# Seven quarter products for eight in the feed-forward stages of a two-block transformer kernel

## The chip, the cores and the metric

The kernel runs on one core of one Trainium2 chip. The metric is device time in microseconds, the median of three runs. The engines of the core are called PE (matrix products; PEld is its loading of weights), DVE (vector), ACT (scalar), POOL (GpSimd) and SP (which here only issues loads).

## The reference

A sequence of 512 tokens of width 1024 goes through two layers of a first block (mixer, then an MLP with a convolution and GELU) and two layers of a second one (feed-forward, mixer, feed-forward). The change is in the four feed-forward stages of the second block:

```python
D_FF_2 = 128 * ((8 * D_MODEL // 3 + 127) // 128)      # 2816

def swiglu(x, w_gate, w_up, w_down):
    return (jax.nn.silu(x @ w_gate) * (x @ w_up)) @ w_down

x = x + 0.5 * swiglu(rms_norm_2(x, norm_ffn1[l]), ffn1_w_gate[l], ffn1_w_up[l], ffn1_w_down[l])
x = x + hybrid_mixer(rms_norm_2(x, norm_mix[l]), ...)
x = x + 0.5 * swiglu(rms_norm_2(x, norm_ffn2[l]), ffn2_w_gate[l], ffn2_w_up[l], ffn2_w_down[l])
```

All of it is in fp32.

## The kernel before

Every dense product is made of three matmuls in float32r. Both operands are split in a high part (a copy rounded by ACT) and a low part (the rest, by DVE), and high x high, high x low and low x high are added up in PSUM (`mm3a`, `mm3b`).

Weights come through `Stream` in chunks of 128 x 1024, in the order of their use. SP loads a chunk into one of three raw buffers; ACT makes `whi` from it (L63), DVE makes `wlo` (L64), into one of four pairs of buffers. `release` frees the pair of a chunk that is used up and at once issues the split of the chunk four places ahead; that split waits until PE has read the old pair.

In a feed-forward stage, the activations lie feature-major in `H`, high and low, 8 blocks of 128 features by 512 tokens. `fm` takes one chunk for 128 output features: 8 blocks x 3 matmuls of 512 columns (L166 to L168). Chunks of gate and up alternate, 44 in all. The first four chunks are done in halves of 256 tokens, since the norm of the last tokens is not ready yet: first all four for tokens 0 to 255, then all four for the rest. `flush` issues, ahead of a half, what is pending for its tokens. `to_h` (L204) turns a token block of 128 by PE and splits it into `H`; block 2 is done as the first half goes on, block 3 at the boundary of the halves. After a gate chunk ACT applies SiLU (L433), after an up chunk DVE multiplies (L437), and the result is split at once into `hid` high and low (L426, L427). Then `finish` makes the down product token-major in two passes of 512 columns (`tm`, L172 to L174), with `hid` as the stationary operand.

The instruction streams of the engines are in the order in which the program issues them (a manual schedule), so whatever is issued to an engine waits for all that was issued to it before. In `fm` the order after a chunk is: evacuation first, then `release`. PSUM has two sets of four banks, tags "a" and "b".

Of the kernel before, what the change touches and what calls it, by code (L numbers as in the profile page):

```python
# [18 lines left out]
L = 2  # L19
# [13 lines left out]

MIX_ORDER = (4, 5, 0, 1, 2, 6, 7, 3)
# [3 lines left out]
class Stream:  # L38
    """Weights in the order of their use: each chunk is loaded, split in two
    float32r parts whose sum it is, and given out."""  # L40

    def __init__(self, nc, raw_pool, split_pool, n_raw, n_split):
        self.nc, self.raw_pool, self.split_pool = nc, raw_pool, split_pool
        self.n_raw, self.n_split = n_raw, n_split
        self.specs, self.raw, self.parts = [], {}, {}
        self.loaded = self.split = self.taken = 0
        self.done = set()
        self.oldest = 0

    def load_ahead(self):  # L50
        while self.loaded < len(self.specs) and self.loaded - self.split < self.n_raw:
            t = self.raw_pool.tile([128, CHUNK], F32, name="wraw")
            self.nc.sync.dma_start(t, self.specs[self.loaded])
            self.raw[self.loaded] = t
            self.loaded += 1

    def split_ahead(self):
        while self.split < len(self.specs) and self.split - self.oldest < self.n_split:
            self.load_ahead()
            t = self.raw.pop(self.split)  # L60
            hi = self.split_pool.tile([128, CHUNK], F32R, name="whi")
            lo = self.split_pool.tile([128, CHUNK], F32R, name="wlo")
            self.nc.scalar.activation(hi, t, AF.Copy)  # L63
            self.nc.vector.tensor_sub(lo, t, hi.bitcast(F32))  # L64
            self.parts[self.split] = (hi, lo)
            self.split += 1
            self.load_ahead()
# [24 lines left out]
class Block:  # L92
    def __init__(self, tc, ctx, a, out):
        self.tc, self.nc, self.a, self.out = tc, tc.nc, a, out
        pool = lambda name, bufs=1, **kw: ctx.enter_context(tc.tile_pool(name=name, bufs=bufs, **kw))
        self.const = pool("const")
        self.keep = pool("keep")
        self.small = pool("small", 4)
        self.gains = pool("gains", 2)
        self.sq = pool("sq", 1)  # L100
        raw, parts = pool("wraw", 3), pool("wparts", 4)
        self.psum = pool("psum", 4, space=bass.MemoryType.PSUM)
        ctx.enter_context(tc.manual_schedule())
# [4 lines left out]
        self.n_half = 4  # L108

# [59 lines left out]

    def mm3b(self, ps, h, w, first, last):  # L170
# [96 lines left out]
    def tm(self, nk, width, rows, evac, tag, tail=0, opens=False):  # L267
        """Token-major products: nk feature blocks against chunks of CHUNK // width
        blocks of width columns each."""
# [11 lines left out]
        for c in range(head):  # L281
# [4 lines left out]
            self.st.release(i)  # L286
        if head == n_chunks:
            for t in range(NT):
                evac(t, ps[t])
            return  # L290
        got = []
        for t in range(NT):
            if opens:
                self.flush(max(self.opened, t))
            for c in range(n_chunks - head):
# [5 lines left out]
                if t == NT - 1 and c == 0:  # L301
                    self.st.release(i)
            evac(t, ps[t])
# [4 lines left out]

    def finish(self, nk, rows, gain, scale=None, post=None, final=False):
        """x += the product of rows with the next weights (scaled, or normed with  # L310
        the gain post), then the next norm's rows on their way to self.H."""
# [40 lines left out]
        def normed(t):  # L352
# [3 lines left out]
            def rows_of_h():  # L356
# [4 lines left out]
                else:  # L361
                    self.later(1800 if t < NT - 1 else math.inf, t, lambda: self.to_h(t, parts, first))
# [3 lines left out]
        self.tm(nk, 512, rows, part0, first)  # L366
        if not final:
            self.new_h()
        self.tm(nk, 512, rows, part1, last, tail=3 if post is None else 4)
# [5 lines left out]
    def begin(self, gain):  # L375
        """The first norm, in the order in which tokens and weights arrive."""
# [95 lines left out]
    def ffn(self, l, next_gain, final):  # L472
        self.mlp(None, next_gain, final)

# [5 lines left out]
    def spare(self, name):  # L480
        """A scratch tile from the slots that the norms use between the stages."""
# [307 lines left out]
    def pooling(self, u, share, pw, gcols, mix):  # L789
        """Means over windows of 2 and 4, then 8 and 16 tokens, by halves."""  # L790
# [133 lines left out]
    def tokens(x, g, t):  # L924
        """The tokens of tile t of group g, of x [p, T]: a run of tokens, or the
        tokens that are t modulo 4, one or four whole residue classes."""
        return x[:, t::4] if g else x[:, t * 128:(t + 1) * 128]

    def dilated(self, half, fm, v, o_dil):
# [4 lines left out]
        for s in range(2):  # L934
# [6 lines left out]
            def near(i):  # L941
                """Scores of key blocks 2i and 2i + 1, each for its own and the next block."""
# [61 lines left out]
            # weights, numerators and denominators  # L1004
# [96 lines left out]
def body(ctx, tc, a, out, stages):  # L1101
    nc = tc.nc
    B = Block(tc, ctx, a, out)
    for kind, l in stages:
        B.st.specs += [a["w_" + kind][l, i] for i in range(N_CHUNKS[kind])]
# [6 lines left out]
    B.begin(gains[0])  # L1112
    for i, (kind, l) in enumerate(stages):
        with tc.tile_pool(name=f"ph{i}", bufs=1) as B.phase:
            f = B.ffn if kind in ("ffn1", "ffn2") else getattr(B, kind)
# [7 lines left out]
def constants():  # L1123
    """Tables that depend on the shapes alone."""
# [40 lines left out]
def tiles_a(w):  # L1165
    """[L, D, N] as chunks [L, N // 128, 128, 8 * 128] of whole columns."""
# [4 lines left out]
def tiles_b(w, width):  # L1171
    """[L, K, N] as chunks [L, (N // width) * (K // 128 // per), 128, per * width]."""
# [5 lines left out]
def arrange(inp):  # L1178
    """The inputs laid out as the program reads them."""
# [12 lines left out]
    def pairs(g, u):  # L1192
        return np.stack([tiles_a(g), tiles_a(u)], axis=2).reshape(L, 2 * KF, 128, CHUNK)
# [3 lines left out]
    for n in ("1", "2"):  # L1197
        a["w_ffn" + n] = np.concatenate([pairs(inp[f"ffn{n}_w_gate_2"], inp[f"ffn{n}_w_up_2"]),
# [43 lines left out]
```

## Time and profile before

| what | value |
|---|---|
| median of three runs | 3565.03 us (3563.9 to 3568.91) |
| span of the profiled execution, first to last instruction | 3553.4 us |
| that execution's own time | the page gives its span alone; the median is 11.6 us above it |
| PE busy | 3500.0 us (98%) |
| DVE, ACT, POOL busy | 43%, 33%, 10% |
| share of PE in the chain that ended last | 93% |

Times in rows are microseconds from the first instruction unless marked ns. A matmul's duration includes its way through the array, and consecutive ones overlap; the distance between starts is what a matmul takes from the next.

### The profile page before, as it was taken

To read this page: it belongs to the slowest core of one execution; us is meant where nothing else is said; L and a number is where in the kernel's file an instruction comes from. 1 tells how busy PE (TensorE), PEld (TensorE's weight loads), DVE (VectorE), ACT (ScalarE), POOL (GpSimd) and SP (SyncE) were. 2 spreads that over 40 slices of the span, in tenths; PEclk is the share of its full clock that TensorE was granted. 3 is DMA by queue.
4 is the path that set the end of the run, shared out by engine and by line. 5 is a ranking of instruction groups with operands and counts; after the bars stand their busy time and mean duration, and the time that the engine had idled before them with its cause. 6 is when DMAs were issued, how large, how long until landed. Compare 5 with 4: busy or idle time off the path is not lost.

```text
span 3553.4 us, 39868 instructions
## 1 busy us (share of the span) xinstructions
PE 3500.0 (98%) x16304; PEld 2842.4 (80%) x16304; DVE 1512.6 (43%) x1973; ACT 1163.3 (33%) x1854; POOL 351.3 (10%) x412
## 2 busy tenths in 40 slices
PE   8999999999999999999999999999999999999999
PEld 6678887767888788889887888888888988788887
DVE  4655542465554343324543533233332454353322
ACT  4344432334443232222235332222222223532222
POOL 2411100241110000002200100000000220010000
PEclk9999999999999999999999999999999999999999
DMA  4123232312223232222111232323222211123232
GB/s 154 47 73 101 95 107 78 110 48 73 100 95 108 76 102 94 101 101 88 49 60 60 89 102 94 104 86 101 94 100 97 88 48 60 61 90 104 92 104 77
DMA packets 87191, 312.00 MB, mean 88 GB/s; under 512 B 10369, under 2 KB 11073, under 8 KB 87009
## 3 DMA queue, kind: packets, MB, share of 16 engines
q1 hardware_dynamic: 85536, 305.17, 25.3%
q0 software_dynamic: 1472, 4.30, 0.4%
q8 instruction: 128, 2.10, 0.2%
q14 instruction: 55, 0.44, 0.0%
HBM read 307.32 MB, written 2.10 MB: 87 GB/s over the span
## 4 chain that ended last, share of the span: by engine, by line
PE 93%; DVE 3%; ACT 1%; POOL 1%; issue 1%; DMA 0%; DVEq 0%; SPq 0%; POOLq 0%; ACTq 0%
PE pa L166 19%; PE pa L167 18%; PE pa L168 18%; PE pb L172 10%; PE pb L173 10%; PE pb L174 10%; PE pst L932 1%; PE pz L1038 1%; PE psc L625 1%; DVE wlo L64 1%; PE ph L209 1%; PE pod L1026 1%; PE pos L1038 1%; PE po L661 1%; DVE pb L343 0%
## 5 line engine op out<-in xcount | busy, mean ns | idle before, releaser
L64 DVE TENSOR_TENSOR wlo<-wraw,whi 128x1024 fp32r<-128x1024 f32 x556 | 708.5, 1277 | 1207.0 <-ACT whi L63 1205.7
L166 PE MATMUL pa<-h_hi,whi 128*128 128x512 f32 (+1 forms) x3072 | 1180.7, 384 | 4.4 <-ACT h_hi L151 4.4
L167 PE MATMUL pa<-h_lo,whi 128*128 128x512 f32 (+1 forms) x3072 | 1158.6, 377 | 5.7 <-DVE h_lo L152 5.7
L168 PE MATMUL pa<-h_hi,wlo 128*128 128x512 f32 (+1 forms) x3072 | 1157.5, 377 | 0.0
L63 ACT ACTIVATE whi<-wraw 128x1024 fp32r<-128x1024 f32 x556 | 583.3, 1052 | 685.4 <-PE pb L174 516.8
L166 PEld LDWEIGHTS pa<-h_hi,whi 128*128 128x128 f32 x3072 | 578.5, 188 | 136.5 <-issue 16.0
L168 PEld LDWEIGHTS pa<-h_hi,wlo 128*128 128x128 f32 x3072 | 578.3, 188 | 117.8
L167 PEld LDWEIGHTS pa<-h_lo,whi 128*128 128x128 f32 x3072 | 579.0, 188 | 116.2 <-DVE h_lo L152 7.9
L172 PE MATMUL pb<-whi,hid_hi 128*128 128x512 f32 x1056 | 413.8, 392 | 0.0
L174 PE MATMUL pb<-whi,hid_lo 128*128 128x512 f32 x1056 | 413.0, 391 | 0.0
L173 PE MATMUL pb<-wlo,hid_hi 128*128 128x512 f32 x1056 | 413.0, 391 | 0.0
L174 PEld LDWEIGHTS pb<-whi,hid_lo 128*128 128x128 f32 x1056 | 198.1, 188 | 43.7
L173 PEld LDWEIGHTS pb<-wlo,hid_hi 128*128 128x128 f32 x1056 | 198.2, 188 | 43.6
L172 PEld LDWEIGHTS pb<-whi,hid_hi 128*128 128x128 f32 x1056 | 198.2, 188 | 43.0
L426 ACT ACTIVATE hid_hi<-act 128x512 fp32r<-128x512 f32 x88 | 55.7, 633 | 396.8 <-DVE act L437 396.8
L190 POOL TENSOR_TENSOR rs<-ss 128x1 f32<-128x1 f32 x44 | 8.8, 200 | 1635.7 <-ACT sqs L180 1635.7
L437 DVE TENSOR_TENSOR act<-act,pa 128x512 f32<-128x512 f32 x88 | 60.5, 688 | 223.3 <-PE pa L168 223.3
L172 PE MATMUL pb<-whi,h_hi 128*128 128x256 f32 (+1 forms) x384 | 142.3, 371 | 2.7 <-ACT whi L63 2.3
L173 PE MATMUL pb<-wlo,h_hi 128*128 128x256 f32 (+1 forms) x384 | 140.0, 365 | 3.9 <-DVE wlo L64 3.9
L446 DVE SCALAR_TENSOR_TENSOR cv<-pa,cw,cv 128x511 f32<-128x511 f32 (+1 forms) x176 | 131.5, 747 | 27.4 <-ACT cv L444 24.3
L174 PE MATMUL pb<-whi,h_lo 128*128 128x256 f32 (+1 forms) x384 | 139.4, 363 | 0.0
L433 ACT ACTIVATE act<-pa 128x512 f32<-128x512 f32 x88 | 52.5, 597 | 259.4 <-PE pa L168 259.3
(229 smaller groups left out, 3011.1 us busy)
## 6 DMA issues: line engine op xcount, KB each, us to landing
wraw<-w_ffn SPq DMA_DIRECT2D x264, 512.0 KB, 3.2
wraw<-w_mix SPq DMA_DIRECT2D x160, 512.0 KB, 3.2
wraw<-w_mlp SPq DMA_DIRECT2D x132, 512.0 KB, 3.2
X<-x SPq DMA_DIRECT2D x4, 512.0 KB, 7.6
gain<-norm_ffn SPq DMA_DIRECT2D x4, 512.0 KB, 4.1
out<-xn SPq DMA_DIRECT2D x8, 256.0 KB, 2.0
gain<-norm_mix_pre SPq DMA_DIRECT2D x2, 512.0 KB, 5.4
rope_da<-c_rope SPq DMA_DIRECT2D x2, 512.0 KB, 8.8
```

Source lines behind the costliest of these rows:

```text
L63: self.nc.scalar.activation(hi, t, AF.Copy)
L64: self.nc.vector.tensor_sub(lo, t, hi.bitcast(F32))
L166: mm(ps, w[0], h[0], start=first, stop=False)
L167: mm(ps, w[0], h[1], start=False, stop=False)
L168: mm(ps, w[1], h[0], start=False, stop=last)
L172: mm(ps, h[0], w[0], start=first, stop=False)
L173: mm(ps, h[0], w[1], start=False, stop=False)
L174: mm(ps, h[1], w[0], start=False, stop=last)
L426: nc.scalar.activation(hid[0][:, f], h, AF.Copy)
L437: nc.vector.tensor_mul(g, g, ps)
L446: nc.vector.scalar_tensor_tensor(c[:, s:], ps[:, :T - s], cw[:, j, i:i + 1], c[:, s:], op0=OP.mult, op1=OP.add)
L1038: mm = lambda out, lhsT, rhs, first: nc.tensor.matmul(out, lhsT, rhs, start=first, stop=True, skip_group_check=True)
```

## The change

Of the 44 gate and up chunks of a stage, the first four stay as they were. The other 40 are done in ten groups of two feature blocks of gate and two of up. A group is a product of a 2 x 2 matrix of weight quarters (gate or up; lower or upper four blocks of input features) with a 2 x 2 matrix of activation quarters (input features by halves, tokens by halves). It is worked out by Winograd's form of Strassen's algorithm: seven products of quarters in place of eight, each of 2 x 4 blocks x 3 matmuls of 256 columns. The sums of weight quarters are made on the chip (`quarter`), and each sum is split like a chunk. The sums of activation quarters are made once a stage (`sums_of_h`, `put`), when token blocks 2 and 3 are turned; for that both are now turned at the boundary of the halves. The products are summed from PSUM by DVE (`seven`). The activations stay in fp32 and are split during the down product, once in each of its two passes.

The weights lie in another order in memory; the number of bytes is the same. Comments and docstrings are removed too. The core of the diff:

```diff
+    def quarter(self, n, which):
+        j, s = which
+        nc = self.nc
+        if j == 0:
+            p = self.halve(self.use(n))
+        elif j == 1:
+            w11, w21, w22 = [self.use(n + i) for i in range(3)]
+            s[1], s[2], s[3] = [self.sum_tile() for _ in range(3)]
+            nc.vector.tensor_add(s[1], w21, w22)
+            nc.gpsimd.tensor_sub(s[3], w11, w21)
+            nc.vector.tensor_sub(s[2], s[1], w11)
+            self.drop(n)
+            self.drop(n + 1)
+            p = self.halve(s[2])
+            nc.gpsimd.tensor_sub(s[2], self.use(n + 3), s[2])
+        elif j == 2:
+            p = self.halve(s.pop(1))
...
     def to_h(self, t, parts, tag):
...
             self.split_to(hi, lo, p)
+            if t >= 2 and self.raw_h is not None:
+                nc.scalar.activation(self.raw_h[0][n, 1][:, :, (t - 2) * 128:(t - 1) * 128], p, AF.Copy)
+        if t >= 2 and self.raw_h is not None:
+            self.raw_h[1](t)
...
+        def put(t):
+            c = slice((t - 2) * 128, (t - 1) * 128)
+            b11, b21, b12, b22 = [raw[i][:, :, c] for i in ((0, 0), (1, 0), (0, 1), (1, 1))]
+            nc.vector.tensor_sub(b11, b12, b11)
+            nc.gpsimd.tensor_sub(b12, b22, b12)
+            nc.vector.tensor_sub(b22, b22, b11)
+            nc.gpsimd.tensor_sub(b21, b21, b22)
+            for i, x in ((2, b22), (1, b11), (3, b12), (4, b21)):
+                self.split_to(T[i][0][:, :, c], T[i][1][:, :, c], x)
...
+    def seven(self, T, tag, evac):
+        def product(ps, first, b):
+            i, w = self.st.take()
+            for j in range(2):
+                for k in range(4):
...
+                    self.mm3q(ps[:, j], [y[:, q:q + 128] for y in w], x, first and j == k == 0)
+                    self.tick(MM3 / 2)
+            self.st.release(i)
...
+        g1, g2 = bank("g1"), bank("g2")
+        product(g1, True, (0, 0))
+        a1, u2 = temp("a1"), temp("u2")
+        nc.scalar.activation(a1, g1, AF.Copy)
+        product(g2, True, 2)
+        add(u2, g2, a1)
+        g5 = bank("g5")
+        product(g5, True, 1)
+        product(g2, False, 3)
+        u3 = temp("u3")
+        add(u3, g2, a1)
+        c2 = self.phase.tile([128, 2, 2, 256], F32, name="c2", tag="act", bufs=1)
+        add(c2[:, :, 1], g5, u3)
+        g4 = bank("g4")
+        product(g4, True, 4)
+        add(c2[:, :, 0], g4, u3)
+        product(g5, False, (1, 1))
+        c12 = temp("c12")
+        add(c12, g5, u2)
+        product(g1, False, (1, 0))
+        evac(g1, c12, c2)
...
-                    self.later(1800 if t < NT - 1 else math.inf, t, lambda: self.to_h(t, parts, first))
+                    inside = t < (2 if self.next_kind in SEVEN else NT - 1)
+                    self.later(1800 if inside else math.inf, t, lambda: self.to_h(t, parts, first))
...
+        def split(n):
+            c = n % (KF // 2)
+            parts[n] = [self.phase.tile([128, 2, 512], F32R, name=f"hid_{s}", tag="t", bufs=8) for s in ("hi", "lo")]
+            self.split_to(*parts[n], hid[c])
+
+        for m in range(1, KF // 2):
...
+            def evac(g1, c12, c2):
+                nc.scalar.activation(x[:, :, :256], g1, AF.Silu)
+                nc.scalar.activation(x[:, :, 256:], c12, AF.Silu)
+                x4 = x.rearrange("p j (h t) -> p j h t", h=2)
+                nc.vector.tensor_mul(x4, x4, c2)
+
+            self.seven(T, tags[m % 2], evac)
...
+        split_next(4)
```

The pair of parts of the split, `halve`, is the `whi` and `wlo` of before.

## Rows read from the trace of the kernel before

**Rows 1.** The page: busy time of the engines; the chain that ended last.
```profile
PE 3500.0 (98%) x16304; PEld 2842.4 (80%) x16304; DVE 1512.6 (43%) x1973; ACT 1163.3 (33%) x1854; POOL 351.3 (10%) x412
...
PE 93%; DVE 3%; ACT 1%; POOL 1%; issue 1%; DMA 0%; DVEq 0%; SPq 0%; POOLq 0%; ACTq 0%
```

**Rows 2.** Windows: half boundary to first down matmul, the four feed-forward stages.
```profile
core 0: us, PE busy (x) PEld busy (x) DVE busy (x) ACT busy (x) POOL busy (x), PEclk, DMA share, GB/s
1253.14:1490.45 237.31, 236.72 (x1067) 192.22 (x1065) 82.80 (x87) 69.64 (x89) 0.00 (x0) 1.00 0.28 96
2035.40:2272.61 237.21, 236.62 (x1067) 192.10 (x1065) 82.89 (x87) 69.67 (x89) 0.00 (x0) 1.00 0.28 96
2406.49:2643.70 237.21, 236.62 (x1067) 192.12 (x1066) 82.79 (x87) 68.43 (x88) 0.00 (x0) 1.00 0.29 96
3188.79:3425.99 237.20, 236.61 (x1066) 192.13 (x1065) 82.76 (x87) 69.74 (x89) 0.00 (x0) 1.00 0.28 95
```

**Rows 3.** Timeline, PE: start us, us; 256 columns, then 512.
```profile
2405.08 0.28 PE L166 MATMUL pa<-h_hi,whi 128*128 128x256 f32 x1
2405.20 0.28 PE L167 MATMUL pa<-h_lo,whi 128*128 128x256 f32 x1
2405.32 0.28 PE L168 MATMUL pa<-h_hi,wlo 128*128 128x256 f32 x1
...
2470.09 0.39 PE L166 MATMUL pa<-h_hi,whi 128*128 128x512 f32 x1
2470.33 0.40 PE L167 MATMUL pa<-h_lo,whi 128*128 128x512 f32 x1
```

**Rows 4.** Groups by form, 2406.49 to 2643.70: busy us, mean ns | idle before.
```profile
L168 PEld LDWEIGHTS pa<-h_hi,wlo 128*128 128x128 f32 x352 | 66.0, 187 | 14.6
...
L64 DVE TENSOR_TENSOR wlo<-wraw,whi 128x1024 fp32r<-128x1024 f32 x43 | 52.7, 1226 | 82.9 <-ACT whi L63 82.9
L63 ACT ACTIVATE whi<-wraw 128x1024 fp32r<-128x1024 f32 x43 | 45.1, 1049 | 5.1 <-PE pa L167 3.2 <-issue 1.3 <-ACT act L433 0.6
...
L437 DVE TENSOR_TENSOR act<-act,pa 128x512 f32<-128x512 f32 x21 | 14.4, 688 | 53.0 <-PE pa L168 53.0
...
L433 ACT ACTIVATE act<-pa 128x512 f32<-128x512 f32 x22 | 13.1, 597 | 64.8 <-PE pa L168 64.8
```

**Rows 5.** Groups by form of POOL, the whole span.
```profile
L453 POOL TENSOR_TENSOR cv<-cv 128x512 f32<-128x512 f32 x44 | 56.9, 1293 | 429.7 <-DVE cv L446 429.7
```

**Rows 6.** Timeline: a weight pair changes hands, 1257.73 to 1259.14.
```profile
1257.73 0.28 PE L167 MATMUL pa<-h_lo,whi 128*128 128x256 f32 x1
...
1257.97 0.28 PE L166 MATMUL pa<-h_hi,whi 128*128 128x256 f32 x1
...
1258.05 1.06 ACT L63 ACTIVATE whi<-wraw 128x1024 fp32r<-128x1024 f32 x1 [3.19 <-PE pa L167]
...
1259.14 1.22 DVE L64 TENSOR_TENSOR wlo<-wraw,whi 128x1024 fp32r<-128x1024 f32 x1 [3.45 <-ACT whi L63]
```

**Rows 7.** Timeline: the boundary of the halves of a feed-forward stage.
```profile
2406.49 1.04 PE L209 MATMUL ph<-ident,xn 128*128 128x128 f32 x8
...
2407.12 1.08 ACT L151 ACTIVATE h_hi<-ph 128x512 fp32r<-128x512 f32 x2 [7.48 <-PE ph L209]
...
2407.76 1.29 DVE L152 TENSOR_TENSOR h_lo<-ph,h_hi 128x512 fp32r<-128x512 f32 x2 [5.11 <-ACT h_hi L151]
...
2407.78 0.39 PE L166 MATMUL pa<-h_hi,whi 128*128 128x256 f32 x1 [0.25 <-ACT h_hi L151]
...
2408.50 0.39 PE L167 MATMUL pa<-h_lo,whi 128*128 128x256 f32 x1 [0.34 <-DVE h_lo L152]
...
2408.72 0.28 PE L168 MATMUL pa<-h_hi,wlo 128*128 128x256 f32 x1
```

**Rows 8.** Timeline: from the last up chunk to the down product.
```profile
2643.46 0.40 PE L168 MATMUL pa<-h_hi,wlo 128*128 128x512 f32 x1
...
2643.70 0.40 PE L172 MATMUL pb<-whi,hid_hi 128*128 128x512 f32 x1
...
2643.89 0.69 DVE L437 TENSOR_TENSOR act<-act,pa 128x512 f32<-128x512 f32 x1 [2.80 <-PE pa L168]
```

**Rows 9.** Timeline: DVE and POOL at the same time, in a mixer stage.
```profile
2789.02 1.28 POOL L489 TENSOR_TENSOR sh<-sh,rope 128x512 f32<-128x512 f32 x1
...
2789.15 2.24 DVE L64 TENSOR_TENSOR wlo<-wraw,whi 128x1024 fp32r<-128x1024 f32 x1
...
2790.38 2.15 POOL L490 TENSOR_TENSOR fmq<-fmq,sh 128x512 f32<-128x512 f32 x1
...
2791.96 0.67 DVE L488 TENSOR_TENSOR fmq<-pa,rope 128x512 f32<-128x512 f32 x1
```

**Rows 10.** Windows: a stop of PE, and what follows it.
```profile
627.84:629.75 1.91, 0.00 (x0) 0.00 (x0) 1.91 (x4) 0.75 (x2) 0.00 (x0) 1.00 0.46 182
629.75:633.20 3.45, 3.45 (x12) 3.05 (x13) 3.42 (x4) 0.69 (x1) 0.00 (x0) 0.51 0.61 203
```

**Rows 11.** The page: loads of weight chunks, us to landing.
```profile
wraw<-w_ffn SPq DMA_DIRECT2D x264, 512.0 KB, 3.2
```

More of the change, by code (lines that the diff above doesn't have):

```diff
@@ L44, in __init__, with add @@
         self.n_raw, self.n_split = n_raw, n_split
-        self.specs, self.raw, self.parts = [], {}, {}
-        self.loaded = self.split = self.taken = 0
+        self.specs, self.raw, self.jobs, self.parts = [], {}, [], {}
+        self.loaded = self.split = self.taken = self.dead = 0
         self.done = set()
         self.oldest = 0
+        self.sum_tile = None
+    def add(self, chunks, quarters=0):
+        for i in range(0, len(chunks), 4 if quarters else 1):
+            n = len(self.specs)
+            self.specs += chunks[i:i + 4] if quarters else chunks[i:i + 1]
+            if not quarters:
+                self.jobs.append((self.plain, n, None))
+            else:
+                sums = {}
+                self.jobs += [(self.quarter, n, (j, sums)) for j in range(7)]
     def load_ahead(self):
-        while self.loaded < len(self.specs) and self.loaded - self.split < self.n_raw:
+        while self.loaded < len(self.specs) and self.loaded - self.dead < self.n_raw:
             t = self.raw_pool.tile([128, CHUNK], F32, name="wraw")
@@ L168, in mm3a, with mm3q @@
         mm(ps, w[1], h[0], start=False, stop=last)
+    def mm3q(self, ps, w, h, first):
+        mm = self.nc.tensor.matmul
+        mm(ps, w[0], h[0], start=first, stop=True, skip_group_check=True)
+        mm(ps, w[0], h[1], start=False, stop=True, skip_group_check=True)
+        mm(ps, w[1], h[0], start=False, stop=True, skip_group_check=True)
     def mm3b(self, ps, h, w, first, last):
@@ L265, in fm_block, with sums_of_h @@
             self.tick(MM3 * n / 512)
[L267 removed]
+    def sums_of_h(self, hid_tile):
+        nc = self.nc
+        quarter = lambda x, n, h: x[:, 4 * n:4 * n + 4, h * 256:(h + 1) * 256]
+        raw = {}
+        for n in range(2):
+            raw[n, 0] = hid_tile().rearrange("p j t -> p (j t)").rearrange("p (k t) -> p k t", k=4)
+            nc.gpsimd.tensor_add(raw[n, 0], quarter(self.H[0], n, 0).bitcast(F32), quarter(self.H[1], n, 0).bitcast(F32))
+            raw[n, 1] = hid_tile().rearrange("p j t -> p (j t)").rearrange("p (k t) -> p k t", k=4)
+        T = {i: [self.phase.tile([128, 4, 256], F32R, name=f"t{i}{s}", tag="t", bufs=8) for s in ("hi", "lo")]
+             for i in (1, 2, 3, 4)}
+        def put(t):
[7 more added lines that the diff above has]
+                self.split_to(T[i][0][:, :, c], T[i][1][:, :, c], x)
+        return T, raw, put
@@ L270, in tm @@
+    def tm(self, nk, width, rows, evac, tag, tail=0, opens=False, release=None):
         per = CHUNK // width
@@ L286, in tm @@
             self.st.release(i)
+            if release:
+                release(c)
         if head == n_chunks:
@@ L302, in tm @@
                     self.st.release(i)
+                if t == NT - 1 and release:
+                    release(head + c)
             evac(t, ps[t])
@@ L472, in ffn, with swiglu, split_next, rows @@
     def ffn(self, l, next_gain, final):
-        self.mlp(None, next_gain, final)
+        nc = self.nc
+        self.st.sum_tile = lambda: self.phase.tile([128, CHUNK], F32, name="wsum", tag="sum", bufs=3)
+        hid_tile = lambda: self.phase.tile([128, 2, 512], F32, name="hid", tag="hid", bufs=KF // 2)
+        T, raw, put = self.sums_of_h(hid_tile)
+        self.raw_h = raw, put
+        hid = [hid_tile()]
+        def swiglu(i, ps):
+            f, up = divmod(i, 2)
+            x = hid[0][:, f]
+            if not up:
+                nc.scalar.activation(x, ps, AF.Silu)
+            else:
+                nc.vector.tensor_mul(x, x, ps)
+        tags = [self.dense_tag, "b" if self.dense_tag == "a" else "a"]
+        self.fm([lambda ps, i=i: swiglu(i, ps) for i in range(4)], halves=True)
+        self.raw_h = None
+        parts = {}
+        def split(n):
[3 more added lines that the diff above has]
+        for m in range(1, KF // 2):
+            x = hid_tile()
+            hid.append(x)
+            def evac(g1, c12, c2):
[4 more added lines that the diff above has]
+            self.seven(T, tags[m % 2], evac)
+        self.dense_tag = tags[KF // 2 % 2]
+        ahead = [0]
+        def split_next(n=1):
+            for _ in range(n):
+                if ahead[0] < KF:
+                    split(ahead[0])
+                    ahead[0] += 1
+        split_next(4)
+        passes = [0]
+        def rows(k, t):
+            return [x[:, k % 2, t * 128:(t + 1) * 128] for x in parts[k // 2 + passes[0]]]
+        def release(c):
+            del parts[c + passes[0]]
+            split_next()
+            if c == KF // 2 - 1:
+                passes[0] = KF // 2
+        self.finish(KF, rows, next_gain, scale=0.5, final=final, release=release)
     def scratch(self, name):
@@ L1104, in body @@
     for kind, l in stages:
-        B.st.specs += [a["w_" + kind][l, i] for i in range(N_CHUNKS[kind])]
+        chunks = [a["w_" + kind][l, i] for i in range(N_CHUNKS[kind])]
+        if kind in SEVEN:
+            B.st.add(chunks[:4])
+            B.st.add(chunks[4:2 * KF], True)
+            B.st.add(chunks[2 * KF:])
+        else:
+            B.st.add(chunks)
     B.ident = B.const.tile([128, 128], F32, name="ident")
```

72 lines of the change are left out of this document (57 added, 15 removed).

## The prediction, made before the changed kernel ran

> **What bounds the kernel now.** I read the engine table and the chain of waits first [rows 1]: TensorE (PE) is busy 98% of the span, and 93% of the chain that ended last is PE. So I went to the stretch that is replaced. There are four SiLU feed-forward stages. In each, the windows view from the transposes in the middle of the first four chunks to the first down-product matmul gives 237.2 us, with PE busy for all but 0.6 us of it and the clock at 1.00 [rows 2]; the reader is to see that the four agree to 0.1 us. In such a stretch the others have room: VectorE (DVE) works 82.8 us, ScalarE (ACT) 68.4 to 69.7, GpSimd (POOL) nothing. Then the timeline: 512-column matmuls start every 0.233 us and 256-column ones every 0.117 us [rows 3], although a weight load is listed with 0.187 us [rows 4]. So halving the columns halves the price, and fewer products are PE time saved, if PE never waits.
>
> **What is removed.** Per stage, 40 of 44 gate and up chunks go through ten groups of `seven`. A group had 4 chunks x 24 matmuls x 0.233 = 22.4 us; it gets 7 products x 24 x 0.117 = 7 x 2.80 = 19.6 us. That is -2.8 us a group, -28.0 a stage, -112 for four. The Trainium skill (TensorE: Matmul & The Clock Gate, Back-to-back issue gap) puts the spacing of warm matmuls at their columns over 2.4 GHz plus 2.5 ns, so 0.216 and 0.109 us; by it a stage would save 10 x (96 x 0.216 - 168 x 0.109) = 24 us, not 28. The rows measure 0.233 and 0.117 and decide. All that follows is what PE has to wait for.
>
> **Load on the other engines.** In a group DVE has seven `lo`, two weight sums and the product with the gate: ten operations on 128x1024 of 1.226 us, and five sums from PSUM priced as the like operation L437 at 0.688 [rows 4]: 12.3 + 3.4 = 15.7 us of 19.6. ACT has 7 x 1.05 + 3 x 0.6 = 9.2. POOL has two 128x1024 operations; the trace has only 128x512 ones, 1.29 us alone [rows 5], so between 1.3 (if the columns cost nothing) and 2.6 (twice); I take 2.45, near twice, because nearly all of 1.29 is columns. No engine is full, so it is the order that decides.
>
> **Waits inside a group.** Each product frees a weight slot, and `product` calls `release` before `seven` issues the sum that reads the bank. So on DVE the sum stands behind the `lo` of the job four ahead, and that waits for ACT's `hi`, which waits for the end of the product. From the rows of such a handover [rows 6], counted from where the next product's first matmul starts (1257.97): `hi` starts at 0.08, `lo` at 1.17 and ends at 2.39. Before, the next chunk took 5.6 us, so this came in time; now a product takes 2.80. The fourth product accumulates into g2, so it waits for u2 (g2 + a1): 2.39 + 0.69 = 3.08, then 0.08 to wake PE and about 0.11 because its weight load isn't ahead (after a wait the next matmul is 0.22 away, not 0.117 [rows 7]): 3.28 - 2.80 = 0.48 us. The sixth accumulates into g5, so it waits for u3 and then for c2's second half: 3.28 + 0.72 = 4.00 - 2.80 = 1.20. Nothing else of the group is late (the first half of c2, c12 and the evacuation work for the other set of banks). 1.68 a group, +16.8 a stage. Bounds: nothing if PE runs on without them, and 1.5 to 2.0 a group if each hop is off by 0.05.
>
> **The half boundary.** Before, block 2 went to H within the first half (1.03 us of transposes) and block 3 at the boundary; the second half ran freely 1.9 us after its transposes began [rows 7]. Now both wait for the boundary, and block 2 takes `put` along before block 3 is looked at. On ACT and DVE, from the first transpose: `hi` at 0.63, two `hi` and two raw copies of 0.54 until 2.8; DVE's first difference 3.0 to 3.7; POOL 1.29 to 5.0; DVE 0.69 to 5.7; POOL to 7.0; four T `hi` of 0.63 on ACT until 8.3, so block 3's first `hi` ends at 8.8; on DVE four T `lo` of 0.69 stand before block 3's `lo`, the first of them held by POOL until about 7.0: they end at 9.7, block 3's at 10.3, and PE runs at 10.5. Against 1.9 + 1.03 = 2.9, that is +7.6 a stage (7 to 9).
>
> **Into the down product.** Before, it follows at the next beat although the last evacuation starts 0.2 us later [rows 8], because that block is needed last. Now the first part of the split activations stands behind the last evacuation. From the end of the last product: one more weight `hi` until 1.1, two SiLU until 2.35, DVE's product 1.23 until 3.6, `hi` 1.05 until 4.7, `lo` 1.23 until 5.95, PE at 6.1: +6.1 a stage (5.5 to 6.5). The split itself (2.5 us of DVE and 2.1 of ACT for 5.6 us of PE) hides after that.
>
> **POOL against DVE.** The rows show that one waits for the other: `lo` issued 0.13 us after a POOL sum took 2.24 instead of 1.23, and the next POOL operation 2.15 instead of 1.29, while the DVE operation that reads PSUM kept its 0.67 beside it [rows 9]. The Trainium skill (GPSIMD Engine Reference, Key points) says that POOL shares its SBUF interfaces with VectorE and contends with instructions of two SBUF inputs; the trace agrees (2.24 against 1.23), and by the rule at its worst all of POOL's 4.9 us would come on top of DVE's 15.7, 20.6 a group, which is under the 21.3 that the waits already make. What it costs: 0 if the two POOL operations of a group fall into DVE's pauses (19.6 + 1.7 - 15.7 = 5.6 us for 4.9), and one hold, 2.45, for each that meets `lo` just before u2 or c2. With the engines laid out in order, the POOL operation that needs the group's last chunk runs beside the next group's first product and the other after the third product, where DVE's waits leave room for most of it: I take 0.05 a group, 0.5 a stage (0 to 1). In the first group DVE is behind already (block 3's `put`, then weight sums): its operations, in order, would hold the second product by 1.5 and the fourth by 3.0 more. I take 2.5 of 0 to 5.
>
> **The clock.** After 1.91 us without a matmul the granted clock was 0.51 for the next 3.45 us, that is the 1.2 GHz level [rows 10]; the stretches with the stops of 0.3 us at the boundary stayed at 1.00 [rows 2, 7]. The two new stops, 8.4 and 6.1 us, are far longer, so I expect half speed after both. It costs half of such a stretch, 1.7 us, at most 3.4 if it is twice as long. At the half boundary DVE's backlog hides it, in the down product nothing does: +1.7 a stage (0 to 3.4).
>
> **Loads and the rest.** A weight chunk lands 3.2 us after its issue [rows 11]. The third of a group's chunks is issued some 6 us before its sum needs it: nothing. The kernel reads the same bytes. The two POOL sums at a stage's start lie under the first half.
>
> **Sum.** Per stage -28.0 + 16.8 + 7.6 + 6.1 + 0.5 + 2.5 + 1.7 = +7.2; four stages +29. The span 3553.4 becomes 3582. The page gives no total for the profiled execution, so its surroundings stay at the median less the span, 3565.0 - 3553.4 = 11.6 (10.5 to 15.5 by the single runs): **3594 us**. With every bound at its low end (7.0, 15.0, 5.5, the rest 0) a stage gets -0.5, 3563; at the high end (9.3 with its clock, 20.0, 6.5, 1.0, 5.0, 3.4) +17.2, 3634.
>
> **Rivals.**
> 1. *PE doesn't wait inside the groups* (faster). It decides at the sixth product: if c2's sum is done within the 2.80 us of the fifth, the waits are 0. For it: DVE has 20% to spare. Against: the handover of [rows 6] alone takes 2.39, and two sums follow. Then a stage gets 7.2 - 16.8 = -9.6, and the time is 3565 - 38 = 3527; without the smaller terms too (0.5, 2.5, 1.7) 3508. Chance 0.14.
> 2. *POOL holds the critical `lo`.* For it: the two-way waiting of [rows 9], at twice the length. Against: it needs POOL's operation just then. One hold of 2.45 in every second group gives +12 a stage, 3594 + 49 = 3643. Chance 0.11.
> 3. *It evens out*: bounds near their low ends, no clock loss and no backlog, as products 1 and 2 find their weights done; 7.2 - 0.5 - 2.5 - 1.7 = 2.5, and shorter hops by 0.1 each make it 0.5: 3567. Chance 0.12.
> 4. *The small matmuls aren't half price*, bound by the weight load: 168 x 0.187 = 31.4 a group against 22.4, +9.0, 40 groups +360, 3925. Against: the run of 256-column matmuls in [rows 3, 6] at 0.117. Chance 0.01.
>
> **How the numbers follow.** The forecast holds 0.62, the rivals the rest. Within 0.2% (7 us, about what a measurement of this kernel can tell from no change) lies most of rival 3: 0.09. Faster: rival 1 and a little of 3: 0.15. Slower: 0.76. The range from 3556 to 3632 holds the forecast's bounds and rival 3, and leaves out rival 1 and most of rival 2.
>
> **What would show it.** Between PE's products: two waits in each group released by DVE, about 0.5 before the second use of g2 and 1.2 before that of g5; a group 21.3 us. At each half boundary 8.4 us of idle PE, at each start of the down product 6.1, each followed by a low clock. `lo` at 1.23 except beside POOL. If groups last 19.6, rival 1 holds; if they last 22 or more with long `lo` right before the waits, rival 2. The stretch of [rows 2] should come out at 237.2 + 1.0 (block 2's transposes are now in it) + 7.2 - 1.7 (the clock, which falls behind it) = 243.7 us; the prediction is wrong in its heart if it is under 237.2.

## The result, and the profile after

| what | before | after |
|---|---|---|
| median of four executions | 3565.3 us (3563.9 to 3568.9) | 3610.4 us (3606.3 to 3611.6) |
| ratio, 95% interval | | 1.0125 (1.011 to 1.0139) |
| span of the profiled execution | 3553.4 us | 3609.2 us |
| that execution's own time | not given | 3611.0 us |

The change makes the kernel 45 us slower; 3594 was forecast, with 3556 to 3632 as the range. The page's engine table and chain of waits, for the same lines as [rows 1]:

```profile
PE 3453.0 (96%) x19184; PEld 2952.1 (82%) x19184; DVE 2034.6 (56%) x2381; ACT 1369.6 (38%) x2062; POOL 611.5 (17%) x516
...
PE 85%; DVE 9%; ACT 3%; issue 1%; POOL 1%; DMA 0%; DVEq 0%; POOLq 0%; ACTq 0%; SPq 0%
```

PE is busy for 47 us less, and yet the span is 56 us longer: PE now waits. DVE's share of the chain has gone from 3% to 9%. The windows of the four stretches of [rows 2], from the first transpose at the half boundary to the first down matmul:

```profile
1266.69:1512.88 246.19, 221.72 (x1795) 217.11 (x1793) 187.58 (x172) 104.10 (x125) 57.59 (x24) 0.97 0.30 93
2058.42:2304.58 246.16, 221.70 (x1795) 217.17 (x1793) 187.94 (x173) 104.10 (x125) 58.58 (x24) 0.97 0.30 93
2440.14:2686.47 246.33, 221.93 (x1794) 217.51 (x1792) 187.66 (x173) 102.67 (x124) 60.01 (x24) 0.97 0.31 93
3232.63:3479.21 246.58, 221.88 (x1795) 217.26 (x1793) 187.87 (x173) 104.09 (x125) 59.34 (x24) 0.97 0.29 93
```

237.2 has become 246.2 to 246.6 (243.7 was forecast), with some 24.5 us in which PE is idle where it was 0.6, and a mean clock of 0.97 where it was 1.00. The waits view of PE in the third stretch names the places (what waited <- for whom: us in total, times, longest us):

```profile
PE g L235 <- DVE c L401: 9.3, 10, 1.0
PE pa L229 <- ACT h_hi L214: 7.4, 1, 7.4
PE g L235 <- DVE u L394: 3.3, 10, 1.8
PE pb L241 <- ACT hid_hi L214: 3.0, 1, 3.0
PE pa L230 <- DVE h_lo L215: 1.0, 1, 1.0
PE pb L243 <- DVE hid_lo L215: 0.9, 1, 0.9
```

There are ten waits for c2's second half (L401) and ten for u2 (L394), one of each in each group. Then come the stop at the half boundary (`pa`) and the one into the down product (`pb`): the three places that the prediction named. One group in the timeline (start us, us; idle before and its releaser in brackets):

```profile
2519.40 0.68 DVE L394 TENSOR_TENSOR u<-g,a 128x512 f32<-128x512 f32 x1
...
2520.23 0.36 PE L235 MATMUL g<-t3hi,whi 128*128 128x256 f32 x1 [0.17 <-DVE u L394]
...
2524.34 1.36 DVE L87 TENSOR_TENSOR wlo<-wraw,whi 128x1024 fp32r<-128x1024 f32 x1 [1.99 <-ACT whi L86]
2525.62 0.68 DVE L399 TENSOR_TENSOR u<-g,a 128x512 f32<-128x512 f32 x1
2526.33 0.69 DVE L401 TENSOR_TENSOR c<-g,u 128x512 f32<-128x512 f32 x1
...
2527.17 0.36 PE L235 MATMUL g<-h_hi,whi 128*128 128x256 f32 x1 [0.97 <-DVE c L401]
```

`wlo` of the block four ahead stands on DVE before the two sums (u3, then c2's second half), and PE's sixth product starts only when both are done. Counted from one matmul's start to the next, the two waits are gaps of 0.45 and 1.23 us where 0.12 is usual.

The half boundary, which answers to [rows 7]:

```profile
2440.14 1.91 PE L278 MATMUL ph<-ident,xn 128*128 128x128 f32 x16
...
2442.13 0.60 ACT L283 ACTIVATE hid<-ph 128x512 f32<-128x512 f32 x1 [0.76 <-DVE h_lo L215]
...
2445.98 0.69 DVE L359 TENSOR_TENSOR hid<-hid 128x512 f32<-128x512 f32 x1 [1.44 <-POOL hid L358]
...
2448.80 0.58 ACT L214 ACTIVATE h_hi<-ph 128x512 fp32r<-128x512 f32 x1
...
2449.42 0.58 PE L229 MATMUL pa<-h_hi,whi 128*128 128x256 f32 x1 [7.37 <-ACT h_hi L214]
...
2451.03 0.58 PE L230 MATMUL pa<-h_lo,whi 128*128 128x256 f32 x1 [1.02 <-DVE h_lo L215]
```

Block 2's `put` goes from DVE to POOL and back. Block 3's first `hi` stands on ACT behind the high parts of `put`'s four sums (T). The second matmul runs 10.9 us after the first transpose. Into the down product, which answers to [rows 8]:

```profile
2684.51 1.22 DVE L87 TENSOR_TENSOR wlo<-wraw,whi 128x1024 fp32r<-128x1024 f32 x1 [0.97 <-ACT whi L86]
...
2685.38 3.89 ACT L214 ACTIVATE hid_hi<-hid 128x1024 fp32r<-128x1024 f32 x4
2685.65 1.22 DVE L657 TENSOR_TENSOR hid<-hid,c 128x1024 f32<-128x1024 f32 x1
...
2686.48 0.50 PE L241 MATMUL pb<-whi,hid_hi 128*128 128x512 f32 x1 [2.98 <-ACT hid_hi L214]
...
2688.06 0.50 PE L243 MATMUL pb<-whi,hid_lo 128*128 128x512 f32 x1 [0.85 <-DVE hid_lo L215]
```

The clock by windows (the columns of [rows 2]): at the half boundary, in the first group behind its longest wait (1.8 us, ended at 2475.85), at the start of the down product, and, last, in a whole later group:

```profile
2446.17:2456.41 10.24, 5.96 (x26) 5.67 (x27) 6.25 (x10) 5.17 (x10) 3.31 (x3) 0.50 0.00 0
2476.30:2479.80 3.50, 3.50 (x21) 3.50 (x20) 0.53 (x1) 0.00 (x0) 1.94 (x1) 0.58 0.62 215
2688.39:2691.81 3.42, 3.42 (x10) 2.66 (x9) 3.02 (x3) 0.88 (x1) 0.00 (x0) 0.52 0.46 189
2511.30:2532.80 21.50, 20.36 (x170) 20.02 (x170) 16.95 (x16) 8.80 (x10) 4.65 (x3) 1.00 0.33 99
```

The first three are the 1.2 GHz level or close to it: at the down product the starts stand 0.427 us apart, where 512 columns take 0.233 otherwise. In the later group, whose two waits are 0.2 and 1.0 us, the clock stayed at 1.00.

The first of the four stages pays for one thing more, in its first half of tokens, while POOL makes the two sums of `h_hi` and `h_lo` (L348):

```profile
1248.77 3.55 DVE L268 SCALAR_TENSOR_TENSOR xn<-X,rs,gain 128x512 f32<-128x512 f32 x2
...
1249.08 5.44 POOL L348 TENSOR_TENSOR hid<-h_hi,h_lo 128x1024 f32<-128x1024 f32 x2
...
1252.25 5.63 DVE L87 TENSOR_TENSOR wlo<-wraw,whi 128x1024 fp32r<-128x1024 f32 x3
...
1255.66 0.58 PE L231 MATMUL pa<-h_hi,wlo 128*128 128x256 f32 x1 [4.14 <-DVE wlo L87]
```

DVE is held twice (`xn` 3.55 us for two, `wlo` 5.63 for three), and PE stops for 4.1 us on a `wlo`; then 256-column matmuls start every 0.21 us until 1261.6.

### The profile page after: what moved, and what is told of

Read it like the earlier page. It is cut to its first block, busy times and chain, and to the rows that moved or that the text cites. A ratio compares the mean times of both kernels' runs of the same rounds, so it can differ in the third digit from the quotient of the medians.

```text
span 3609.2 us, 46818 instructions
## 1 busy us (share of the span) xinstructions
PE 3453.0 (96%) x19184; PEld 2952.1 (82%) x19184; DVE 2034.6 (56%) x2381; ACT 1369.6 (38%) x2062; POOL 611.5 (17%) x516
## 4 chain that ended last, share of the span: by engine, by line
PE 85%; DVE 9%; ACT 3%; issue 1%; POOL 1%; DMA 0%; DVEq 0%; POOLq 0%; ACTq 0%; SPq 0%
PE pb L243 10%; PE pb L241 10%; PE pa L229 10%; PE pb L242 10%; PE pa L230 10%; PE pa L231 10%; PE g L235 7%; PE g L236 6%; PE g L237 6%; DVE wlo L87 3%; ACT whi L86 2%; PE pst L1140 1%; PE pz L1246 1%; PE psc L833 1%; DVE c L401 1%
## 5 line engine op out<-in xcount | busy, mean ns | idle before, releaser
L229 PE MATMUL pa<-h_hi,whi 128*128 128x512 f32 (+1 forms) x1792 | 681.6, 380 | 32.8 <-ACT h_hi L214 32.8
L230 PE MATMUL pa<-h_lo,whi 128*128 128x512 f32 (+1 forms) x1792 | 659.5, 368 | 8.5 <-DVE h_lo L215 8.5
L231 PE MATMUL pa<-h_hi,wlo 128*128 128x512 f32 (+1 forms) x1792 | 658.1, 367 | 4.1 <-DVE wlo L87 4.1
L229 PEld LDWEIGHTS pa<-h_hi,whi 128*128 128x128 f32 x1792 | 345.4, 193 | 106.0 <-ACT h_hi L214 36.0
L231 PEld LDWEIGHTS pa<-h_hi,wlo 128*128 128x128 f32 x1792 | 344.9, 192 | 63.8 <-DVE wlo L87 4.3
L230 PEld LDWEIGHTS pa<-h_lo,whi 128*128 128x128 f32 x1792 | 345.6, 193 | 60.8 <-DVE h_lo L215 11.0
L235 PE MATMUL g<-h_hi,whi 128*128 128x256 f32 x960 | 271.1, 282 | 37.1 <-DVE c L401 37.1
L87 DVE TENSOR_TENSOR wlo<-wsum,whi 128x1024 fp32r<-128x1024 f32 x160 | 269.0, 1683 | 59.9 <-ACT whi L86 59.7
L236 PE MATMUL g<-h_lo,whi 128*128 128x256 f32 x960 | 268.0, 279 | 0.0
L237 PE MATMUL g<-h_hi,wlo 128*128 128x256 f32 x960 | 267.9, 279 | 0.0
```

Source lines behind the costliest of these rows:

```text
L229: mm(ps, w[0], h[0], start=first, stop=False)
L230: mm(ps, w[0], h[1], start=False, stop=False)
L231: mm(ps, w[1], h[0], start=False, stop=last)
L235: mm(ps, w[0], h[0], start=first, stop=True, skip_group_check=True)
L236: mm(ps, w[0], h[1], start=False, stop=True, skip_group_check=True)
L237: mm(ps, w[1], h[0], start=False, stop=True, skip_group_check=True)
```

## The experiments

All start from the changed kernel; the ratio is to the kernel before, the interval is 95%. The code cuts show the core of each edit; "..." marks what is left out.

| edit | median us | ratio, interval |
|---|---|---|
| the change itself | 3610.4 | 1.0125 (1.011 to 1.0139) |
| 1. sum before the split | 3544.7 | 0.9943 (0.9928 to 0.9959) |
| 2. both blocks turned first | 3599.6 | 1.0093 (1.0076 to 1.011) |
| 3. down product's parts split early | 3586.4 | 1.0055 (1.0039 to 1.0071) |
| 4. first-half sums on DVE | 3607.2 | 1.0116 (1.0099 to 1.0134) |
| 5. edits 1, 3, 4 | 3518.0 | 0.9862 (0.9847 to 0.9877) |
| 6. edits 1, 2, 3, 4 | 3504.2 | 0.9827 (0.9813 to 0.9842) |
| 7. weight sums on DVE, alone | 3608.8 | 1.0114 (1.0099 to 1.0129) |
| 8. edits 1, 3, 4, 7 | 3513.1 | 0.9854 (0.9837 to 0.987) |
| 9. edits 1, 2, 3, 4, 7 | 3504.0 | 0.9824 (0.9811 to 0.9838) |
| 10. as 9, the boundary's sums on DVE too | 3496.6 | 0.9807 (0.9794 to 0.9821) |

**1. The sum before the split.** What reads a bank is issued before `release` issues the next split, for all seven products: DVE's sums, and with them ACT's copy a1 and the evacuation:

```diff
-        def product(ps, first, b):
+        def product(ps, first, b, then):
...
+            then()
             self.st.release(i)
...
-        product(g2, True, 2)
-        add(u2, g2, a1)
+        product(g2, True, 2, lambda: add(u2, g2, a1))
```

> Change: in each of the seven products the sum that reads the bank is issued ahead of the release of the weight pair, so ahead of the next split on DVE and ACT. Theory A (the waits inside a group come from the order, DVE's sum standing behind the split): the wait before the second use of g5 (1.1 us) goes, that before g2's falls to 0.5 or less, a group goes from 21.5 to 19.7 to 20.2 us, and the time from 3610 to 3540 to 3560. Theory B (DVE and POOL are simply full in a group): the group stays at 21 or more, the time within 15 us of 3610. Theory C (the split is what is late next, since it now stands behind the sums): waits of 1 us or more for a weight's low part take their place, 3590 to 3610.

Measured: -65.7 us. A group takes 20.0 us in place of 21.5, and among PE's waits in the third stage none is left on c2 and one on u (0.7 us, in the first group):

```profile
PE pa L229 <- ACT h_hi L214: 7.4, 1, 7.4
PE pb L241 <- ACT hid_hi L214: 3.1, 1, 3.1
PE g L237 <- DVE wlo L87: 1.2, 2, 0.7
PE pa L230 <- DVE h_lo L215: 1.0, 1, 1.0
PE g L235 <- DVE u L393: 0.7, 1, 0.7
PE pb L243 <- DVE hid_lo L215: 0.4, 1, 0.4
```

So the order of issue made the waits, not DVE's load: DVE has the same 2381 operations in both. This edit alone turns the sign.

**2. Both blocks turned first.** Raw copies and `put` of both blocks are issued after both are split into `H`:

```diff
             if t >= 2 and self.raw_h is not None:
-                nc.scalar.activation(self.raw_h[0][n, 1][:, :, (t - 2) * 128:(t - 1) * 128], p, AF.Copy)
-        if t >= 2 and self.raw_h is not None:
-            self.raw_h[1](t)
+                self.turned.append((n, t, p))
+        if t == 3 and self.raw_h is not None:
+            raw, put = self.raw_h
+            for n, u, p in self.turned:
+                nc.scalar.activation(raw[n, 1][:, :, (u - 2) * 128:(u - 1) * 128], p, AF.Copy)
...
+            put(2)
+            put(3)
```

> Change: at the boundary of the halves both token blocks are turned and split into H first; the raw copies and the sums of activation quarters of both blocks follow. Theory A (the boundary is a symptom: DVE's work from the boundary to the end of the first group is the limit, wherever it waits): the second half starts at about 3.3 us after the transposes in place of 10.9, but the first group's products then wait some 6 us for weights; the stage gains 1 to 4 us, 3594 to 3606 in all. Theory B (the boundary stop is a cost of its own): the stage gains the whole 7.6 and the low clock behind it, 8 to 10 us, 3570 to 3578 in all.

Measured: -10.8 us. The second matmul of the second half runs 3.2 us after the first transpose in place of 10.9, but the first group takes 29.5 to 31.1 us in place of 25.4. New among its waits, third stage:

```profile
PE g L238 <- DVE wlo L87: 4.2, 3, 3.4
PE g L236 <- ACT whi L86: 1.7, 1, 1.7
```

Most of the stop moves to where the weight splits stand behind the boundary's work; 2.7 us a stage are gained, as theory A said.

**3. The down product's parts split early.** The first two hidden parts are split after the fifth product of the last group:

```diff
         add(c2[:, :, 0], g4, u3)
+        if early:
+            early()
         product(g5, False, (1, 1))
...
-            self.seven(T, tags[m % 2], evac)
+            self.seven(T, tags[m % 2], evac, (lambda: split_next(2)) if m == KF // 2 - 1 else None)
...
-        split_next(4)
+        split_next(2)
```

> Change: the first two parts of the activations for the down product are split after the fifth product of the last group, in place of after its evacuation. Theory A (the down product waits only because the split stands behind the last evacuation): the stop of 4.6 us at its start goes, and the low clock behind it (1.5 us); the rest is as it was; 3583 to 3590. Theory B (DVE is late there anyway, so the work just moves in front of c12 and the down weights' low parts): half of it comes back as a wait for a weight's low part, 3596 to 3605.

Measured: -24.0 us, 6.0 a stage. The last group goes from 24.5 to 21.4 us, the third matmul of the down product runs 0.47 us after the first (1.6 before), and PE's waits between the third stage's boundary and down product have none for `hid_hi` or `hid_lo`. The slow clock goes with the stop: in the same place the granted clock is 1.00 (2672.65 to 2676.07).

**4. The first half's sums on DVE.** The two sums L348 are made by DVE, 4 us into the first half by the program's own count of dense work (in the first stage's trace 9.3 us behind the half's first matmul):

```diff
-            nc.gpsimd.tensor_add(raw[n, 0], quarter(self.H[0], n, 0).bitcast(F32), quarter(self.H[1], n, 0).bitcast(F32))
...
+        def first_half():
+            for n in range(2):
+                nc.vector.tensor_add(raw[n, 0], quarter(self.H[0], n, 0).bitcast(F32), quarter(self.H[1], n, 0).bitcast(F32))
...
+        self.later(4000, 2, first_half)
```

> Change: the two sums of high and low of the first half's activations, on POOL at the start of a stage, are made by DVE some 4.4 us into the first half. Theory A (POOL's two sums, 2.7 us each, keep DVE from its weight split): in the first feed-forward stage PE's stop of 4.1 us for a low weight part and the low clock behind it go; 7 us of that stage, nothing in the other three: 3600 to 3606. Theory B (that stop is the luck of one execution, or comes with the norm of the last block): 3608 to 3613.

Measured: -3.2 us, which the spread of the runs does not tell from nothing; 3607.2 lies between the ranges of the two theories. The trace does show the effect, in the first stage: its first half, from the transposes ahead of it to the boundary's, is 5.8 us shorter, and both groups of DVE operations that POOL had held are back to their length:

```profile
1250.31 1.41 DVE L268 SCALAR_TENSOR_TENSOR xn<-X,rs,gain 128x512 f32<-128x512 f32 x2
1251.63 3.49 DVE L87 TENSOR_TENSOR wlo<-wraw,whi 128x1024 fp32r<-128x1024 f32 x3
```

**5. Edits 1, 3 and 4 together.** No other code.

> Three edits at once on the changed kernel: each product's sum issued before the next weight block's split, the down product's first two hidden parts split after the fifth product of the last group, and the first half's two sums of h_hi and h_lo on DVE in place of POOL. Theory A (the three stops are separate, so their gains add): alone they measured 3544.7, 3586.4 and 3607.2 us against 3610.4, that is gains of 65.7, 24.0 and 3.2 us by the times; by the traces the stops they take out were 15 a stage, 4.6 plus the low clock behind it a stage, and 5.8 us once. Sum: 3510 to 3520 us; the groups stay at 20.0 us, the last one falls from 23.26 to about 20.0, the way from the first turning of the half boundary to the down product's first matmul is about 226 us. Rival B (the early split takes DVE's time in the last group, which the sum issued first has just freed, and the sums on DVE meet the first weight splits): the last group stays above 22 us and the time above 3525.

Measured: 3518.0, which is 3610.4 less the three gains (92.9) to 0.5 us, closer than the spread of the runs lets one expect. All groups, the last with them, take 20.0 us (one 20.1) but for the first (22.0 to 22.5); the stretch of [rows 2] is 226.2 us. The three stops are separate.

**6. With edit 2 too.**

> The three edits of the run before, and both token blocks of the half boundary turned and split before the raw copies and sums of either. Theory A (DVE's backlog behind the boundary sets the first group, and turning both first moves the stop from the boundary into it): alone this edit gave 10.8 us over four stages (3610.4 to 3599.6) and with the sums issued first the first group has less to wait for, so 5 to 15 us less than the run before: 3497 to 3512 us, the second half's second matmul at 3.2 us behind the first turning, the first group 26 to 30 us. Rival B (the backlog costs the same wherever it stands): within 3 us of the run before.

Measured: 13.9 us less than the run before. The stretch is 223.6 us; the first group takes 27.3.

**7. The weight blocks' differences on DVE.**

```diff
-            nc.gpsimd.tensor_sub(s[3], w11, w21)
+            nc.vector.tensor_sub(s[3], w11, w21)
...
-            nc.gpsimd.tensor_sub(s[2], self.use(n + 3), s[2])
+            nc.vector.tensor_sub(s[2], self.use(n + 3), s[2])
```

> The changed kernel with the two differences of weight blocks that POOL makes in each group (2.83 and 2.55 us, one holding the other engine up) made by DVE instead; nothing else is different. Theory A (while POOL does such an operation, DVE's operation that runs beside it on SBUF is held for as long as POOL has the port, so DVE loses beside POOL about what it would need to do the operation itself: the splits of the summed blocks take 1.68 us on the mean where a split alone takes 1.23, four in a group, 1.8 us, and others besides, against 2 x 1.22 = 2.4 us of added work): DVE's lo of a summed block falls to about 1.23 us, the groups stay at 21.5 us within 0.4, and the time stays within 10 us of 3610. Rival B (the two engines overlap, and DVE, already behind, gets 2.4 us more in each of 40 groups): groups at 22.5 to 23.9 us, time 3650 to 3700.

Measured: 3608.8 against 3610.4, the same. `wlo` of summed blocks by the view of its line, first of the changed kernel, then of this one (x160: shortest/median/longest ns):

```profile
L87 DVE TENSOR_TENSOR wlo<-wsum,whi x160: 1207/1226/3244, 1292.8 to 3461.6; 128x1024 fp32r<-128x1024 f32 x160
```

```profile
L87 DVE TENSOR_TENSOR wlo<-wsum,whi x160: 1211/1217/1229, 1292.1 to 3450.6; 128x1024 fp32r<-128x1024 f32 x160
```

DVE took over 80 operations (97 us), and its busy time on the page is 2033.7 us, where it was 2034.6: the time in which POOL held it was as long as the work. Between the first group and the last the groups stay at 21.4 to 21.8 us. Only in the first group is DVE done sooner: it takes 22.2 to 22.3 us in three of four stages, and the wait for u2 that was 1.8 us long there is gone (third stage; the longest is now 0.5):

```profile
PE g L235 <- DVE u L394: 2.1, 9, 0.5
```

The median does not show this gain of some 10 us in four stages. The profiled execution took 3599.9 us, the other three 3608.8 to 3609.2; they have no trace, so whether their first groups were shorter too is open.

**8. Edits 1, 3, 4 and 7.**

> The three edits of the first run of this set, and the weight blocks' differences on DVE as in the run before. Theory A (DVE has slack in a group once the sums are issued first, and is held by POOL for about as long as the work takes): groups at 20.0 us as without it, the first groups within 1 us, the time within 5 us of the first run of this set. Rival B (2.4 us more of DVE's time a group brings a wait back): groups at 20.5 us or more, 20 us or more lost over 40 groups.

Measured: 4.9 us less than without edit 7, about as much as single runs differ. Groups at 20.0 us but for a few (the longest 21.5, behind a wait of 1.2 us for u). The first ones take 20.1 to 21.2 in place of 22.0 to 22.5, in three stages a larger change than theory A's 1 us.

**9. All four edits and edit 7.**

> The four edits together (3504.2 us), and the differences of weight blocks on DVE in place of POOL, which gave -1.6 us on the changed kernel and -4.9 us on the one with three edits. Theory A (in the first group DVE is late because of its own backlog and because POOL's sums hold its splits there): the first group of each stage falls from 27.3 us by 0.5 to 2 us, the other groups stay at 20.0, and the time is 3496 to 3503 us. Rival B (with both blocks turned first, the first group waits for the boundary's raw copies and splits alone, in which POOL's weight sums have no part): the first group stays at 27.3 within 0.3 and the time within 3 us of 3504.

Measured: 3504.0 against 3504.2: no difference in time. The first group did fall, by 1.7 us (25.6 to 25.7), as theory A said; its time (3496 to 3503) is just missed. The four stretches of [rows 2] together are 4.5 us shorter than in run 6; in the first stage a later group lasts 21.6 us with a wait of 1.2 us for DVE. What took the gain back lies outside them, where both runs do the same work: the first boundary comes 1.6 us later, and the way from the third stage's first down matmul to the fourth's boundary is 2.9 us longer. The cause of that stays open.

**10. The boundary's differences on DVE as well.**

```diff
-            nc.gpsimd.tensor_sub(b12, b22, b12)
+            nc.vector.tensor_sub(b12, b22, b12)
             nc.vector.tensor_sub(b22, b22, b11)
-            nc.gpsimd.tensor_sub(b21, b21, b22)
+            nc.vector.tensor_sub(b21, b21, b22)
```

> The run before, and the two differences of activations that POOL makes for each token block at the half boundary made by DVE as well (128x512 each). In the traces DVE sits idle 1.5 us before its second difference, since POOL's takes 1.3 us and more where DVE's takes 0.69, and a split beside POOL's second one took 1.23 in place of 0.68, or 2.85 for one. Theory A (the chain from the boundary to the first product runs through DVE and POOL in turns, so DVE alone is done sooner): the first group falls by 2 to 4 us a stage against the run before, 8 to 15 us in all, time 3484 to 3492 us. Rival B (the chain runs through ACT's raw copies and eight splits, so DVE's part does not set it): within 3 us of the run before.

Measured: 7.4 us less, where theory A gave 8 to 15. The first group starts 14.4 us after the first transpose in place of 16.3; it is not shorter itself (25.2 to 25.6). So the chain through POOL was part of the stop. The waits that remain are for ACT and DVE; the longest of PE's, third stage:

```profile
PE g L236 <- ACT whi L86: 1.7, 1, 1.7
PE g L238 <- DVE wlo L87: 1.5, 2, 0.8
PE g L236 <- DVE u L404: 0.7, 1, 0.7
```

This is the fastest version: 68 us (1.9%, by the interval 1.8 to 2.1) under the kernel before. The seven products do pay, once PE does not wait for them.

## Why the prediction was right, and by how much its terms were off

Direction and cause held: fewer matmuls, and waits that eat more than these give. That the sum came so close is in part luck, since terms that were off by 2 to 4 us a stage offset each other. Per stage (the last three; the first stands below), in us:

| term | predicted | measured | from |
|---|---|---|---|
| fewer matmuls | -28.0 | -24.0 | ten groups of 20.0 (run 1, no waits) for 22.4 |
| waits in the groups, with POOL's holds | +17.3 | +15.0 | 21.5 less 20.0, ten times |
| half boundary, to its second matmul | +7.6 | +7.9 | 10.9 less (2.0 + 1.03) |
| clock behind it | 0 | +2.3 | first group starts 24.3 after the first transpose, 14.2 would be before's (13.2, and 1.03 for block 2's transposes); less 7.9 |
| first group | +2.5 | +3.9 | 25.4 less 21.5 |
| into the down product | +6.1 | +4.1 | last group 24.5 less 21.5, and 1.1 at the third matmul |
| clock there | +1.7 | +1.7 | 3.42 us at 0.52 |
| sum | +7.2 | +10.9 | what the traces give, between the last down matmuls of one product and the next: 10.6 to 10.9 |

- **Price of a matmul.** 256 columns start every 0.119 us, not 0.117 (168 in 20.0 us without a wait, run 1). I halved 0.233 where the three starts in [rows 3] already stood 0.12 apart; in 168 matmuls that is 0.4 us. The Trainium skill (TensorE: Matmul & The Clock Gate, Back-to-back issue gap) has a fixed cost per matmul beside the columns; by that formula 168 small ones are to 96 large ones as 0.885 to 1. Measured is 20.0 to 22.4, 0.893, and my halving gave 0.875. The traces' spacings (0.233 and 0.119) are 8% and 9% above the formula's (0.216 and 0.109), but that small matmuls aren't quite half price, as it has them, the traces confirm: the 24 us a stage that the prediction set aside for its own 28 is what was measured. The prediction left out that the Trainium skill, in that section, calls this the gap of isolated matmuls and puts a stream of 512-column matmuls with weight loads at about 131 ns each; the traces here, at 233 ns, don't agree with that.
- **Waits.** The chain of [rows 6] held to within 0.1 us. A product is 2.86 us long, not 2.80, so each wait is 0.06 shorter, the same error with the other sign: a group is 21.5, forecast 21.3. Of the 0.5 a stage for POOL's holds nothing is seen: without POOL's operations the groups are as long (run 7).
- **Half boundary.** The stop was right to 0.3 us. That DVE's backlog would hide the low clock was wrong: it lasts 10.2 us, 7.0 of them after PE's first matmul, and PE has a whole half of matmuls to do before it waits for anything else.
- **First group.** The waits themselves were 2.1 us more than in the other groups, forecast 2.5. The low clock comes on top: 3.5 us at 0.58 behind a wait of 1.8 us, some 1.5 us; together 3.6 of the 3.9. POOL's weight sums are behind most of it: in run 7's trace, without them, the first group is 22.2 to 22.3 us in three stages.
- **Into the down product.** Too high by 2.0: I let the first part's `hi` wait for the last group's product with the gate. That product belongs to the last part; in the trace the first `hid_hi` (2685.38) starts before it (2685.65), and right behind SiLU.
- **The step that failed** is "The two POOL sums at a stage's start lie under the first half". In the first stage they held DVE, and PE with it, and this stage came out 17.9 us longer than before, 7 more than the others. I had priced what POOL does in the groups and not there, though [rows 9] showed the holding. Run 4 took 5.8 of it back.
- **The surroundings.** 11.6 us were taken for what lies around the span. It is 1.8 (3611.0 less 3609.2). The rest was that the profiled execution of before was some 10 us faster than its median: up to the first feed-forward stage the work is the same, and yet the last token block ahead of the MLP before it is turned at 855.3 in the one and 862.8 in the other. As a step from that execution to the median the number served, by another cause than the text gave: luck.

So 3594 is 16 under 3610. The four stages came out 50.3 us longer, where 29 was forecast: 21 too little, 7 of it in the first stage. The other way go some 5 us that stay open: the unchanged stages are 5.6 us longer in the profile after than in that of before (55.9 us at the last down matmul less the 50.3), not the 10 that the medians would have.

## What to carry to other kernels

When a stage is cut into smaller products, the time of an engine that follows each product must be laid out in its order of issue, not by its load: DVE had a fifth of its time free in a group (busy 16.95 of 21.5 us) and still set the pace, and one line moved ahead of another was worth 66 us. A sum that frees a bank for the next product goes ahead of preparation for a later one. Look for a low clock behind each long stop of PE, and count it as part of the stop's price. In the feed-forward stages of the changed kernel it followed every stop of 1.8 us or more; two stops of 1.9 us elsewhere in the same trace (ended at 235.2 and 1235.5) were not followed by one.

## What the runs showed of the hardware

- DVE and POOL on SBUF operands took turns by nearly whole operations. In run 1:

```profile
2497.48 2.41 POOL L109 TENSOR_TENSOR wsum<-wraw,wsum 128x1024 f32<-128x1024 f32 x1 [6.64 <-DVE wlo L87]
2497.86 3.11 DVE L87 TENSOR_TENSOR wlo<-wsum,whi 128x1024 fp32r<-128x1024 f32 x1
```

`wlo` starts 0.4 us after POOL's operation and ends 1.1 us after it, nearly its whole length alone (1.23). POOL needs 2.4 us for what DVE does in 1.22 (run 7), so here an operation given to POOL relieved DVE of nothing where the two met.
- ACT's raw copy waited 0.76 us for DVE's `h_lo`, which reads the same PSUM tile (2442.13): two readers of one tile ran one after the other. Whether the chip or the program's waits ask for it wasn't tried.
